# Three pairs of feature tiles in seven products in each later part's Down, with scratch tiles reused, and one unit's plain products moved

## Chip, cores and metric

One core of a Trainium2 chip. The metric is the device time of one launch in microseconds (us), less is better. TensorE (PE) multiplies, VectorE (DVE) and ScalarE (ACT) do elementwise work, GpSimd (POOL) does some of it too and issues a few DMAs, SyncE (SP) issues most DMAs.

## The reference

A trunk of two layers over 512 positions and 1024 features, float32, batch 1. Each layer has two gated feed-forwards with a mixer between them:

```python
for l in range(2):
    x = x + 0.5 * swiglu(rms_norm(x, ffn1_norm[l]), ffn1_w_gate[l], ffn1_w_up[l], ffn1_w_down[l])
    h = rms_norm(x, mix_norm[l])
    a, g, q, k, v = split(h @ w_in[l])
    # causal depthwise convolution of width 31 on a * sigmoid(g); two softmax maps of q, k with a
    # shared position bias, A1 - lam * A2, lam from four vectors lambda_q1, k1, q2, k2
    x = x + concatenate([conv_out, diff_out]) @ w_out[l]
    x = x + 0.5 * swiglu(rms_norm(x, ffn2_norm[l]), ffn2_w_gate[l], ffn2_w_up[l], ffn2_w_down[l])

def swiglu(h, w_gate, w_up, w_down):        # 1024 -> 2816 -> 1024
    return (silu(h @ w_gate) * (h @ w_up)) @ w_down
```

## The kernel before

**Layout and products.** x lies feature-major: 8 tiles of 128 features by 512 positions. Every product is made in three matmuls: weights and data are each split into a rounded part (hi, an ACT copy) and what is left (lo, a DVE subtraction), and hi·hi, hi·lo and lo·hi are summed in PSUM. Weights come by SP's DMAs into a ring (wraw), and their hi and lo into two more (whi, wlo).

**A feed-forward.** Its 2816 inner features are 22 tiles, split by PARTS into three parts. The first, 5 tiles, is done plainly: 512 columns a matmul, lines 138 to 142. The parts of 8 and 9 tiles are done in units, all of whose matmuls come from line 377. `Unit.body` writes out the order; the scheduler may interleave it. There are two kinds:

- A GateUp unit makes one inner tile: the gate and up products, as one two-by-two block product (two weight blocks for gate and for up, two halves of the positions) with seven half-width products in place of eight (the scheme of Strassen and Winograd), 84 matmuls of 256 columns. Its weights are u1, u2, g1, g2 (halves of a DMA'd tile each), and four sums of them, which POOL makes (lines 354 to 357). The first of these sums goes into a tile of the ring wraw2, called "D". The operands A, B, C and D of a unit are: u (its first half replaced by u1+u2), g, the two last sums, and the first sum.
- A Down unit makes two output tiles A = 2q and B = 2q+1 (q = 0 to 3, four units for a part). `pairs` pairs of the part's inner tiles are taken in seven half-width products each, the others plainly with 512 columns: for B into a bank of its own (`spare`, tile ps_d), for A into the unit's second bank (`plain(self.banks[1], 0)`).

**Order in a unit.** On PE a unit runs: c (weights u2u1, data t1), d (u2, t4), for Down with q > 0 the spare products, then the `rest` of the unit before (g1u1, t3), a (g1, b11), b (g2, b21), `middle` (Down's plain products for A), c (all, b22), a (g1u2u1, t2), `close`. The last of the a-products is read out by ACT into a keep copy (line 426) before `rest`, issued in the next unit, may add to the same bank. Within a unit the next one's weights are made: hi of A, B, D, C on ACT (line 363), lo on DVE (line 367), from sums that POOL made ahead.

**The data of Down.** `Gated` takes a finished GateUp tile: a hi copy (line 628) and lo (line 633), and for the first tile of a pair a held copy in float32 (line 613) and a half-tile subtraction (line 618). When the second of a pair is there, `combine` (lines 635 to 648) makes three sums of the pair and their hi and lo, into scratch named by STORE: two slots of ht, one of rb, and s0 to s2. `Halves` makes the sums of the feed-forward's input, with the same ht slots as its scratch.

**Ends.** The last Down unit of a feed-forward is followed by its `rest` and then by the mixer, by the next feed-forward, or by the end of the kernel. The call `after` starts the statistics of the next norm for an output tile, or the output's DMA.

**The start.** While x is loaded, `make_scalars` fetches the four lambda vectors of each layer (tile lamv, POOL's queue) and forms lam. `make_bias` fetches the onehot table (tile oneh, in the ring sq of two slots, which also holds the squares of the first norm).

Of the kernel before, what the change touches and what calls it, by code (L numbers as in the profile page):

```python
# [41 lines left out]
HS = SEQ // 2  # L42


PARTS = ((0, 5, 0), (5, 8, 2), (13, 9, 2))
PLAIN = PARTS[0][1]
PIN = False

# [20 lines left out]
def trunk(ctx: ExitStack, tc: tile.TileContext, xt, par, lamv, relb, onehot,  # L69
          gu1, dn1, wag, wqkv, wout, gu2, dn2, out):  # L70
    nc = tc.nc
    V, S, G, T = nc.vector, nc.scalar, nc.gpsimd, nc.tensor
# [14 lines left out]
    def bank(tag, name):  # L87
        return psum.tile([P, 512], F32, tag=tag, name=name, bufs=BANKS[tag])


    RING = {"wraw": 5, "whi": 4, "wlo": 4, "wraw2": 2, "whi2": 2, "wlo2": 2}

    def ring(tag, n=1024):
        dt = F32 if "raw" in tag else F32R
        return wp.tile([P, n], dt, tag=tag, name=tag, bufs=RING[tag])

# [197 lines left out]
    class Halves:  # L294
# [4 lines left out]
        def __init__(self, fp, pr, r):  # L299
            self.th = fp.tile([P, 3, KT // 2, HS], F32R, tag="th", name="th")  # L300
            self.tl = fp.tile([P, 3, KT // 2, HS], F32R, tag="tl", name="tl")

            self.whole = []
            free = [f"{t}{n}" for t in ("hh", "hl") for n in range(5, 9)]
            a, b = slice(0, HS), slice(HS, SEQ)
            for j in range(KT // 2):
                for k in (j, j + KT // 2):
                    h = fp.tile([P, SEQ], F32, tag=free.pop(), name="hn")
                    V.scalar_tensor_tensor(h, x[:, k, :], col(pr.l, pr.gain, k), r, op0=ALU.mult, op1=ALU.mult)
                    self.whole.append((k, h))  # L310
# [22 lines left out]
    def pinned(ins, pin=PIN):  # L333
        if pin:
            tc.keep_in_program_order(ins)
        return ins
# [4 lines left out]
    def by_two(t):  # L341
        return t.rearrange("p (n c) -> p n c", n=2)
# [150 lines left out]
    class Down(Unit):  # L493
# [6 lines left out]
        def load(self):  # L500
            A, B = 2 * self.q, 2 * self.q + 1
            whole, over, J = min(self.many, 8), max(self.many - 8, 0), self.steps * P

            def pull(raw, at, m, k, end):
                while k < end:
                    half, f = divmod(self.m0 + k, HALF)
                    b, w = m * HALF + f, 1
                    while (b + w) % 8 and k + w < end and f + w < HALF:
                        w += 1
                    c = b % 8  # L510
                    nc.sync.dma_start(raw[:, at : at + w * P], self.dn[half, b // 8][:, c * P : (c + w) * P])
# [18 lines left out]
            self.cols = {"A": whole * P, "B": whole * P, "C": 2 * J, "D": J + 2 * over * P}  # L530

        def weights(self, wt, j):
            k, b = {"u2u1": ("A", 2 * j), "u2": ("A", 2 * j + 1), "g1": ("B", 2 * j), "g2": ("B", 2 * j + 1),
# [4 lines left out]
            return self.h.get(xt, j)  # L538

        def plain(self, ps, n, first=False):  # L540
            over = max(self.many - 8, 0)
            w = [
                self.w("BA"[n], k) if k < 8 else self.w("D", self.steps + n * over + k - 8)
                for k in range(2 * self.steps, self.many)
            ]
            self.product(ps, zip(w, self.h.hh[2 * self.steps :]), first)

        def spare(self):
            self.ps = bank(("tp", "y")[self.q % 2], "ps_d")
            self.plain(self.ps, 1, first=True)  # L550
# [14 lines left out]
        def close(self):  # L565
            A, B = 2 * self.q, 2 * self.q + 1
            two, keep = by_two(self.banks[1]), self.keep
            if not self.early_free:
                self.plain(self.banks[1], 0)
            pinned(V.tensor_tensor(two, two, keep[:, 0::2], op=ALU.add))  # L570
# [4 lines left out]
            two = by_two(self.ps)  # L575
            pinned(V.tensor_tensor(two, two, keep[:, 1::2], op=ALU.subtract))
            self.into(B, two, 0.5)

        def rest(self):
            self.go(self.a, "g1u1", "t3")  # L580
            B = 2 * self.q + 1
            self.into(B, self.a.unsqueeze(1).broadcast_to([P, 2, HS]), -0.5)
            self.after(B)

    class Gated:

        STORE = (("ht", "ht", "rb"), ("s0", "s1", "s2"))

        def __init__(self, fp, pairs):
            self.fp, self.pairs = fp, pairs  # L590
            self.hh, self.sums, self.held = [], [], {}

        def part(self, tag):
            pool, bufs = (act, None) if tag == "rb" else (self.fp, 2 if tag == "ht" else None)
            return pool.tile([P, SEQ], F32R, tag=tag, name="hs", **({"bufs": bufs} if bufs else {}))

        def plain(self, n, us):
            hi = self.fp.tile([P, SEQ], F32R, tag=f"hh{n}", name="hh")
# [8 lines left out]
        def add(self, n, us, step):  # L607
            a, b = slice(0, HS), slice(HS, SEQ)
            first = self.paired(n) and n % 2 == 0
            if step == 0:  # L610
                if first:
                    self.held[n] = self.fp.tile([P, SEQ], F32, tag=("hh8", "hl8")[n // 2 % 2], name="hold")
                    pinned(S.activation(self.held[n], us, AF.Copy))
                else:
                    self.part_hi(n, us)
            if step == 1:
                if first:
                    pinned(V.tensor_tensor(us[:, b], self.held[n][:, a], self.held[n][:, b], op=ALU.subtract))
# [16 lines left out]
        def combine(self, n, us):  # L635
            if not self.paired(n) or n % 2 == 0:
                return
            a, b = slice(0, HS), slice(HS, SEQ)
            t = self.held[n - 1]
            pinned(V.tensor_tensor(t[:, b], us[:, b], t[:, b], op=ALU.subtract))  # L640
            pinned(V.scalar_tensor_tensor(t[:, a], t[:, a], -1.0, t[:, b], op0=ALU.mult, op1=ALU.subtract))
            pinned(V.scalar_tensor_tensor(us[:, a], us[:, a], -1.0, t[:, a], op0=ALU.mult, op1=ALU.subtract))
# [553 lines left out]
```

## Time and profile before

| what | value |
|---|---|
| median of 3 runs | 1791.06 us (1789.68 to 1792.72) |
| the profiled execution | 1787.99 us, of which the span is 1786.2 |
| matmul records | 11437 |
| POOL busy | 950.4 us, 53% of the span |
| weight DMAs of GateUp | 172 of 512 KB, 3.6 us each to landing |
| DMA, mean over the span | 100 GB/s |

Times of instructions come from the one profiled execution, which is shorter than each of the timed runs. A row of the chain gives start, length, engine, tile and line, and the number of instructions that follow one another (x12). A row of the timeline gives start, length, engine, line, operation, the tile written, the tiles read, shapes, and in brackets how long the engine was idle before it and for what. Matmuls are pipelined: what one costs in a stream is the length of a piece over its count, not the duration of a record.

### The profile page before, as it was taken

Reading aid. Unit: us, or ns where it says so; the run is one execution under the profiler, and the core shown is the slowest. Engines: PE = TensorE matmul, PEld = TensorE weight load, DVE = VectorE, ACT = ScalarE, POOL = GpSimd, SP = SyncE. Lnnn points to the kernel's source line nnn. Section 1 sums busy time; section 2 is a strip of 40 time slices with the busy share of each in tenths; the row PEclk is TensorE's granted clock in tenths of the full one; section 3 lists DMA queues with packets and bytes.
Section 4 is the critical chain, followed back from the end, with each engine's and each line's share of the span. In section 5 each row is a group of like instructions: output and inputs, shape, how many; then the busy total and the mean of one; then the engine's idle time right before and its main releaser. Section 6 shows DMA issues by size and latency. Waiting matters only on the chain.

```text
span 1786.2 us, 29641 instructions
## 1 busy us (share of the span) xinstructions
PE 1771.4 (99%) x11437; PEld 1608.5 (90%) x11437; DVE 1416.0 (79%) x1949; ACT 960.1 (54%) x1555; POOL 950.4 (53%) x665
## 2 busy tenths in 40 slices
PE   9999999999999999999999999999999999999998
PEld 7899999888788899999888999998877888999997
DVE  6988797768857978798668978976788588887974
ACT  5455465545844456465534654655558354554652
POOL 2275475279952166475304745742798432654750
PEclk9999999999999999999999999999999999999999
DMA  7333334423122233333332333344230232333332
GB/s 224 95 113 97 105 107 113 128 91 95 48 71 83 83 95 118 85 113 120 107 97 71 107 107 99 103 119 130 71 116 26 72 106 73 106 97 105 107 108 70
DMA packets 74222, 177.83 MB, mean 100 GB/s; under 512 B 8951, under 2 KB 30726, under 8 KB 74080
## 3 DMA queue, kind: packets, MB, share of 16 engines
q1 hardware_dynamic: 72480, 174.10, 31.9%
q8 instruction: 89, 1.46, 0.3%
q0 software_dynamic: 1312, 1.67, 0.3%
q14 instruction: 53, 0.43, 0.1%
q10 hardware_dynamic: 288, 0.16, 0.0%
HBM read 173.79 MB, written 3.42 MB: 99 GB/s over the span
## 4 chain that ended last, share of the span: by engine, by line
PE 96%; DVE 2%; ACT 1%; issue 0%; DMA 0%; SPq 0%; DVEq 0%; ACTq 0%
PE ps_pair L377 53%; PE ps_d L377 6%; PE ps_pair L141 5%; PE ps_pair L142 5%; PE ps_pair L138 5%; PE ps_d L138 2%; PE ps_d L142 2%; PE ps_d L141 2%; PE ps_sc L966 2%; PE ps_pair L842 2%; PE ps_pair L843 2%; PE ps_pair L844 2%; PE ps_out L138 1%; PE ps_out L142 1%; PE ps_out L141 1%; PE ps_v L872 1%
## 5 line engine op out<-in xcount | busy, mean ns | idle before, releaser
L367 DVE TENSOR_TENSOR wlo<-wraw,whi 128x1024 fp32r<-128x1024 f32 (+2 forms) x400 | 534.6, 1342 | 122.0 <-ACT whi L363 120.2
L363 ACT ACTIVATE whi<-wraw 128x1024 fp32r<-128x1024 f32 (+2 forms) x400 | 361.5, 909 | 354.6 <-PE ps_pair L377 188.3
L354 POOL TENSOR_TENSOR wraw<-wraw 128x512 f32<-128x512 f32 (+1 forms) x100 | 145.1, 1451 | 540.9 <-DMA wraw<-in_gu 279.4
L377 PE MATMUL ps_pair<-acth,wlo 128*128 128x256 f32 x1088 | 307.9, 283 | 0.0
L377 PE MATMUL ps_pair<-actl,whi 128*128 128x256 f32 x1088 | 307.9, 283 | 0.0
L377 PE MATMUL ps_pair<-acth,whi 128*128 128x256 f32 x1088 | 307.9, 283 | 0.0
L377 PE MATMUL ps_pair<-th,whi 128*128 128x256 f32 x816 | 231.7, 284 | 0.0
L377 PE MATMUL ps_pair<-th,wlo 128*128 128x256 f32 x816 | 230.9, 283 | 0.0
L377 PE MATMUL ps_pair<-tl,whi 128*128 128x256 f32 x816 | 230.9, 283 | 0.0
L377 PEld LDWEIGHTS ps_pair<-acth,whi 128*128 128x128 f32 x1088 | 208.9, 192 | 0.2
L377 PEld LDWEIGHTS ps_pair<-actl,whi 128*128 128x128 f32 x1088 | 208.9, 192 | 0.2
L377 PEld LDWEIGHTS ps_pair<-acth,wlo 128*128 128x128 f32 x1088 | 208.9, 192 | 0.0
L101 ACT ACTIVATE whi<-wraw 128x1024 fp32r<-128x1024 f32 (+3 forms) x124 | 122.6, 999 | 144.4 <-PE ps_pair L141 87.3
L141 PE MATMUL ps_pair<-actl,whi 128*128 128x512 f32 x448 | 174.7, 391 | 0.7 <-DVE actl L227 0.5
L142 PE MATMUL ps_pair<-acth,wlo 128*128 128x512 f32 x448 | 174.1, 390 | 0.0
L138 PE MATMUL ps_pair<-acth,whi 128*128 128x512 f32 x448 | 173.2, 392 | 0.4 <-ACT whi L101 0.4
L356 POOL TENSOR_TENSOR wraw<-wraw 128x512 f32<-128x512 f32 (+1 forms) x100 | 154.0, 1540 | 7.8
L377 PEld LDWEIGHTS ps_pair<-th,whi 128*128 128x128 f32 x816 | 156.6, 192 | 0.9
L357 POOL TENSOR_TENSOR wraw<-wraw 128x512 f32<-128x512 f32 (+1 forms) x100 | 153.2, 1532 | 7.8
L377 PEld LDWEIGHTS ps_pair<-tl,whi 128*128 128x128 f32 x816 | 156.6, 192 | 0.0
L377 PEld LDWEIGHTS ps_pair<-th,wlo 128*128 128x128 f32 x816 | 156.6, 192 | 0.0
L355 POOL TENSOR_TENSOR wraw<-wraw 128x512 f32<-128x512 f32 (+1 forms) x100 | 148.1, 1481 | 7.8
(203 smaller groups left out, 4307.5 us busy)
## 6 DMA issues: line engine op xcount, KB each, us to landing
wraw<-in_gu SPq DMA_DIRECT2D x172, 512.0 KB, 3.6
wraw<-in_wqkv SPq DMA_DIRECT2D x24, 512.0 KB, 3.6
wraw<-in_wag SPq DMA_DIRECT2D x16, 512.0 KB, 3.6
wraw<-in_wout SPq DMA_DIRECT2D x16, 512.0 KB, 3.6
wraw<-in_dn SPq DMA_DIRECT2D x60, 128.0 KB, 3.0
wraw<-in_dn SPq DMA_DIRECT2D x20, 384.0 KB, 3.3
wraw<-in_dn SPq DMA_DIRECT2D x28, 256.0 KB, 2.9
wraw<-in_dn SPq DMA_DIRECT2D x20, 320.0 KB, 3.1
```

The lines of the kernel that those rows point to most:

```text
L101: S.activation(hi, raw, AF.Copy)
L138: first = T.matmul(ps, wh, xh, start=start, stop=False)
L141: T.matmul(ps, wh, xl, start=False, stop=False)
L142: T.matmul(ps, wl, xh, start=False, stop=stop)
L354: G.tensor_tensor(d, g1, u1, op=ALU.add)
L355: G.tensor_tensor(u1, u1, u2, op=ALU.add)
L356: G.tensor_tensor(m0, u1, g1, op=ALU.add)
L357: G.tensor_tensor(m1, m0, g2, op=ALU.add)
L363: pinned(S.activation(hi[:, : self.cols[k]], self.raw[k][:, : self.cols[k]], AF.Copy), pin)
L367: pinned(V.tensor_tensor(out=lo[:, :c], in0=self.raw[k][:, :c], in1=f32(hi[:, :c]), op=ALU.subtract), pin)
L377: mm = T.matmul(ps, l, r, start=first and i == n == 0, stop=False, skip_group_check=True)
L842: T.matmul(ps[n], xh[:, t], wh, start=k == 0, stop=False)
```

## The change

- Both later parts take three pairs of inner tiles in seven products, where it was two: six of 8 and six of 9 tiles, so that two and three tiles stay plain.
- The scratch for the third pair's sums comes from tiles that exist: ht becomes one tile of three slots (`Halves` uses parts of it in turn), then rb, s0 to s4 follow, in order of demand. The list goes on with slots of ssum and sq, which three pairs don't reach.
- The ring wraw2 has one slot, where it had two.
- The ninth tile's weight columns: A's stay in D behind its sums; B's no longer fit there, since 3 + 2 tiles are more than 512 columns, and go behind the sums in C.
- In the last unit of a feed-forward, A's plain products move from `middle` to `close`, that is behind the t2 products and ahead of `rest`.
- The half-tile subtraction for the first of a pair reads one operand from PSUM, not from the held copy.
- lamv takes the slots of sq, not one of its own.
- The guards and the branch for parts that have no plain tile are never taken with these sizes.

By the order in which the changed kernel's instructions stand on each engine, the matmuls of 256 columns grow by 672 and those of 512 shrink by 384. ACT, DVE and POOL keep their order but for the added operations of the third pair. On POOL's queue the two lamv DMAs stand directly ahead of the first one of oneh, and on DVE their two reductions stand between the lo subtractions of the first weights, the second directly ahead of line 200's reduction.

```diff
-PARTS = ((0, 5, 0), (5, 8, 2), (13, 9, 2))
+PARTS = ((0, 5, 0), (5, 8, 3), (13, 9, 3))
...
-    RING = {"wraw": 5, "whi": 4, "wlo": 4, "wraw2": 2, "whi2": 2, "wlo2": 2}
+    RING = {"wraw": 5, "whi": 4, "wlo": 4, "wraw2": 1, "whi2": 2, "wlo2": 2}
...
+            ht = fp.tile([P, 2, 3, HS], F32, tag="ht", name="ht")
             for j in range(KT // 2):
...
-                t = fp.tile([P, 3, HS], F32, tag="ht", name="ht", bufs=2)
+                t = ht[:, j % 2]
...
-            pull(d, J, A, whole, self.many)
-            pull(d, J + over * P, B, whole, self.many)
             more = ring("wraw")
+            at = {"D": J, "C": 2 * J}
+            raw = {"D": d, "C": more}
+            where = ("D", "D") if J + 2 * over * P <= 512 else ("D", "C")
+            self.ninth = []
+            for n, m in enumerate((A, B)):
+                k = where[n]
+                self.ninth.append((k, at[k] // P))
+                pull(raw[k], at[k], m, whole, self.many)
+                at[k] += over * P
...
         def middle(self):
-            if self.early_free:
+            if self.early_free and not self.last:
                 self.plain(self.banks[1], 0)
...
-            if not self.early_free:
+            if not self.early_free or self.last:
                 self.plain(self.banks[1], 0)
...
-        STORE = (("ht", "ht", "rb"), ("s0", "s1", "s2"))
...
+        def part(self):
+
+            if not self.slots:
+                ht = self.fp.tile([P, 3, SEQ], F32R, tag="ht", name="hs")
+                self.slots = [lambda n=n: ht[:, n] for n in range(3)]
+                tags = [(act, "rb", None)] + [(self.fp, f"s{n}", None) for n in range(5)]
+                tags += [(tmp, "ssum", 1), (tmp, "sq", None), (tmp, "sq", None)]
...
+            return self.slots.pop(0)()
...
-                    pinned(V.tensor_tensor(us[:, b], self.held[n][:, a], self.held[n][:, b], op=ALU.subtract))
+                    pinned(V.tensor_tensor(us[:, b], self.held[n][:, a], us[:, b], op=ALU.subtract))
...
-            hi, lo, four = (self.part(tag) for tag in self.STORE[n // 2])
+            hi, lo, four = (self.part() for _ in range(3))
...
-            t = tmp.tile([P, SEQ], F32, tag="diag", name="lamv", bufs=1)
+            t = tmp.tile([P, SEQ], F32, tag="sq", name="lamv")
```

More of the change, by code (lines that the diff above doesn't have):

```diff
@@ L529, in load @@
             self.raw = {"A": u, "B": g, "C": more, "D": d}
-            self.cols = {"A": whole * P, "B": whole * P, "C": 2 * J, "D": J + 2 * over * P}
+            self.cols = {"A": whole * P, "B": whole * P, **at}
         def weights(self, wt, j):
@@ L540, in plain @@
         def plain(self, ps, n, first=False):
-            over = max(self.many - 8, 0)
+            if 2 * self.steps == self.many:
+                return
             w = [
-                self.w("BA"[n], k) if k < 8 else self.w("D", self.steps + n * over + k - 8)
+                self.w("BA"[n], k) if k < 8 else self.w(*self.ninth[n])
                 for k in range(2 * self.steps, self.many)
@@ L548, in spare @@
         def spare(self):
-            self.ps = bank(("tp", "y")[self.q % 2], "ps_d")
-            self.plain(self.ps, 1, first=True)
+            if 2 * self.steps < self.many:
+                self.ps = bank(("tp", "y")[self.q % 2], "ps_d")
+                self.plain(self.ps, 1, first=True)
         def early(self):
@@ L574, in close @@
                 self.spare()
-            two = by_two(self.ps)
-            pinned(V.tensor_tensor(two, two, keep[:, 1::2], op=ALU.subtract))
-            self.into(B, two, 0.5)
+            if 2 * self.steps < self.many:
+                two = by_two(self.ps)
+                pinned(V.tensor_tensor(two, two, keep[:, 1::2], op=ALU.subtract))
+                self.into(B, two, 0.5)
         def rest(self):
@@ L581, in rest @@
             B = 2 * self.q + 1
-            self.into(B, self.a.unsqueeze(1).broadcast_to([P, 2, HS]), -0.5)
+            if 2 * self.steps < self.many:
+                self.into(B, self.a.unsqueeze(1).broadcast_to([P, 2, HS]), -0.5)
+            else:
+                pinned(V.tensor_tensor(self.d, self.a, self.keep[:, 3], op=ALU.add))
+                pinned(V.tensor_tensor(self.a, self.a, self.keep[:, 1], op=ALU.add))
+                self.into(B, by_two(self.banks[0]), -0.5)
             self.after(B)
     class Gated:
-        STORE = (("ht", "ht", "rb"), ("s0", "s1", "s2"))
         def __init__(self, fp, pairs):
             self.fp, self.pairs = fp, pairs
[L591 to L595, printed above, removed]
+            self.hh, self.sums, self.held, self.slots = [], [], {}, []
+        def part(self):
[4 more added lines that the diff above has]
+                tags += [(tmp, "ssum", 1), (tmp, "sq", None), (tmp, "sq", None)]
+                self.slots += [
+                    lambda pool=pool, tag=tag, bufs=bufs: pool.tile(
+                        [P, SEQ], F32R, tag=tag, name="hs", **({"bufs": bufs} if bufs else {}))
+                    for pool, tag, bufs in tags
+                ]
+            return self.slots.pop(0)()
         def plain(self, n, us):
```

## The prediction

> **What bounds the kernel now.** I read the page first: its first part (busy time of each engine) and the shares of the chain that ended last.
>
> ```profile
> span 1786.2 us, 29641 instructions
> PE 1771.4 (99%) x11437; PEld 1608.5 (90%) x11437; DVE 1416.0 (79%) x1949; ACT 960.1 (54%) x1555; POOL 950.4 (53%) x665
> PE 96%; DVE 2%; ACT 1%; issue 0%; DMA 0%; SPq 0%; DVEq 0%; ACTq 0%
> ```
>
> TensorE is busy for 99% of the span and makes up 96% of the chain. So the change is worth what it saves on PE, plus the few PE stalls it closes, minus those it opens. Next the chain in order of time, for the price of both matmul widths and for the stalls:
>
> ```profile
> 90.65 87.87 PE ps_pair L377 x720
> 178.52 2.72 PE ps_d L377 x12
> ...
> 185.42 7.77 PE ps_pair L377 x54
> ...
> 328.87 3.43 PE ps_d L377 x15
> ...
> 344.18 6.91 PE ps_pair L377 x44
> 351.15 1.06 ACT whi L101
> 352.21 0.28 ACT keep L426
> 352.54 0.98 PE ps_pair L377 x6
> ...
> 1238.25 1.06 ACT whi L101
> ```
>
> The ps_d pieces are 512-wide plain products: 2.72/12 = 0.2267 us and 3.43/15 = 0.2287 us; I take 0.228. The first piece is 720 matmuls, of which 12 are plain products of the first Down unit and 708 are 256-wide: (87.87 − 2.72)/708 = 0.1203 us. The x54 piece is 42 half-width and 12 plain ones: 42 × 0.1203 + 12 × 0.228 = 7.79, and it took 7.77, so both prices hold in a mixed stream. No piece of another engine stands between these until 351.09 (344.18 + 6.91): there PE waits until 352.54 for ACT, which first makes the hi part of the mixer's next weights (1.06 us) and only then the keep copy (0.28 us) that Down's rest products need. The second layer shows the same piece at 1238.25.
>
> How much room the others have, in one stretch of GateUp and one of Down units (columns: window, length, then busy time with instruction count of PE, PEld, DVE, ACT, POOL, then clock, DMA share, GB/s):
>
> ```profile
> 213.00:303.00 90.00, 90.00 (x753) 90.00 (x752) 80.86 (x92) 54.54 (x86) 57.48 (x36) 1.00 0.38 113
> 303.00:351.00 48.00, 48.00 (x293) 43.01 (x291) 32.79 (x43) 25.40 (x41) 14.65 (x13) 1.00 0.35 109
> ```
>
> DVE is at 90% in GateUp and 68% in Down, POOL at 64% and 31%.
>
> **The third pair.** Two more feature tiles of a part go from plain to seven products. For one Down unit (two output tiles) that removes 2 tiles × 2 outputs × 3 = 12 matmuls of 512 columns and adds 7 × 3 = 21 of 256: 21 × 0.1203 = 2.526 against 12 × 0.228 = 2.736, a gain of 0.21 us. There are 4 units × 2 parts × 4 feed-forwards = 32: **−6.7 us**. With 0.2267 or 0.2287 for the wide ones it is −6.2 or −7.0. All of it is on PE, so on the path.
>
> Here a page of the Trainium skill speaks against the change. "TensorE: Matmul & The Clock Gate", section "Back-to-back issue gap", gives for a stream of weight loads and matmuls about 81 ns at 128 columns and about 131 ns at 512, so narrow products would be far from half price. An estimate from that page, by a straight line 98 ns for 256, makes it 21 × 98 − 12 × 131 = +0.49 us a unit, 15 us slower in all. The trace does not agree: 0.1203 and 0.228 us, nearly half price, and the rows decide.
>
> **The moved last products.** In the last unit of a feed-forward A's plain products (now 9: three tiles × 3) go from before the b22 and t2 products to behind t2. At both FFN1 ends they take 9 × 0.228 = 2.05 us, which is longer than the 1.45 us that PE waits there now; the copies are made meanwhile. −1.4 each, **−2.8**. If ACT came later still, up to 0.6 us of it would be covered too. The price: A's own sum now starts at the end of these products, 0.65 us behind where the keep copy ends, so the mixer's statistics of that tile come that much later (0 to +0.5 each, taken as 0, since PE has the rest products and the mixer's first plain products to do). Layer 0's FFN2 has no wait there: its rest products start without an idle remark, behind products of the next feed-forward.
>
> ```profile
> 900.42 0.40 PE L377 MATMUL ps_pair<-hs,whi 128*128 128x256 f32 x2
> ```
>
> So 0 for it. At the kernel's end the chain is
>
> ```profile
> 1780.46 0.39 ACT keep L426
> 1780.88 0.71 DVE ps_pair L570
> 1781.62 0.69 DVE x L561
> 1782.31 0.60 DVEq L1191
> ```
>
> Last products of t2 to the last update of x: 2.47 us (1780.44 to 1782.91). Afterwards t2 ends earlier by 15 plain matmuls moved or dropped for A and 6 dropped for B (21 × 0.228 = 4.79), later by 18 half-width ones of this unit and 3 of the previous rest (21 × 0.1203 = 2.53): −2.26. From there: 2.05 of plain products, then on DVE the sum (0.71) and two updates of x (0.69, 0.60), with the gaps of some hundredths between the rows 4.1 in place of 2.47: +1.63. Together −0.63, of which 0.2 stands already among the 32 units: **−0.4**.
>
> **lamv in the ring of sq.** At the start the two lamv tiles lay in a slot of their own; now they take the two slots of sq, are fetched only when the sums of squares are made, and the onehot tile, which has the same ring, must wait until they are read.
>
> ```profile
> 27.39 0.57 POOL L740 DMA_DIRECT2D oneh<-in_onehot  x1 [11.07 <-DVE ssum L239]
> 27.95 4.63 DVE L102 TENSOR_TENSOR wlo<-wraw,whi 128x1024 fp32r<-128x1024 f32 x4
> 32.49 0.69 DVE L200 TENSOR_REDUCE rowv<-ps_rows 128x4 f32<-128x512 f32 x1
> 33.47 1.04 POOL L189 TENSOR_TENSOR rs_y<-rowv,mhalf 128x4 f32<-128x4 f32 x1 [5.51 <-DVE rowv L201]
> 37.06 0.65 PE L209 MATMUL ps_spread<-ident,rs_y 128*128 128x128 f32 x4
> L761 POOL TENSOR_TENSOR lamv<-lamv x4: 309/317/322, 6.1 to 16.0; 128x64 f32<-128x64 f32 x4
> L763 DVE TENSOR_REDUCE lamd<-lamv x2: 273/279/285, 7.0 to 16.3; 128x2 f32<-128x128 f32 x2
> DMA to landing us min/median/max: 4.3/5.4/6.5
> ```
>
> The first lamv DMA issues where oneh does now, 27.39, and lands at 31.7 to 33.9; two POOL products and one reduction are 0.9. Its reduction stands on DVE between the second and the third of the four wlo, so those two (2.3 us) start after 32.6 to 34.8 and end at 34.9 to 37.1; then come the second reduction (0.28) and L200, now at 32.49, at 35.2 to 37.4: 2.7 to 4.9 later. From L200 to ps_spread there are 2.5 us of slack (rs_y ends at 34.51, PE uses it at 37.06). So PE waits 0.2 to 2.4 us, once; I take the middle, **+1.3**. Queued behind on POOL are the oneh DMAs and rs_y, on DVE the two wlo for PE's next products: all in the same wait, and paid once.
>
> **One wraw2 slot in place of two.** The "D" sums of unit n+2 (L354, POOL) may now start only when lo of D of unit n+1 (L367, DVE) has read the slot. The stretch of two GateUp units:
>
> ```profile
> 232.20 1.06 ACT L363 ACTIVATE whi<-wraw 128x1024 fp32r<-128x1024 f32 x1 [0.41 <-PE ps_pair L377]
> 242.28 1.06 ACT L363 ACTIVATE whi<-wraw 128x1024 fp32r<-128x1024 f32 x1 [1.32 <-POOL wraw L356]
> 243.25 0.37 ACT L426 ACTIVATE keep<-ps_pair 128x256 f32<-128x256 f32 x1
> 237.60 1.50 DVE L367 TENSOR_TENSOR wlo<-wraw,whi 128x512 fp32r<-128x512 f32 x1
> 244.05 1.21 DVE L367 TENSOR_TENSOR wlo<-wraw,whi 128x1024 fp32r<-128x1024 f32 x1
> 246.72 2.31 DVE L367 TENSOR_TENSOR wlo<-wraw,whi 128x1024 fp32r<-128x1024 f32 x1
> 249.62 1.12 DVE L367 TENSOR_TENSOR wlo<-wraw,whi 128x512 fp32r<-128x512 f32 x1
> 237.25 1.29 POOL L354 TENSOR_TENSOR wraw<-wraw 128x512 f32<-128x512 f32 x1 [3.77 <-DMA wraw<-in_gu]
> 238.62 1.62 POOL L355 TENSOR_TENSOR wraw<-wraw 128x512 f32<-128x512 f32 x1
> 248.03 2.17 POOL L355 TENSOR_TENSOR wraw<-wraw 128x512 f32<-128x512 f32 x1
> ...
> 325.87 0.69 DVE L367 TENSOR_TENSOR wlo<-wraw,whi 128x512 fp32r<-128x512 f32 x1 [0.82 <-ACT whi L363]
> ```
>
> A unit lasts 10.08 us (232.20 to 242.28). In the second one a pair of tiles is combined for Down, in the first not; I call them combining and light. lo D ends 6.9 us after the unit's start in the first (239.10), 8.5 in the second (250.74). L354 and L355, on which the next unit's hi A waits, take 3.0 to 3.5. Unmoved, the sums would be ready at 9.9 to 10.4 and 12.0. But the two sides now overlap: a 1024-wide lo takes 1.21 alone and 2.31 beside POOL, the 512-wide one 0.69 and 1.12 to 1.50. With the sums behind lo D, lo B and lo D run alone: about 0.8 less in the light unit (6.1) and 1.5 less in the combining one, of which about 1 is given back, since the later sums run into the next lo A (1.21 to 2.3): 8.0. So ready at 9.1 to 9.6 and 11.0 to 11.5. hi A, 1.06, and behind it on ACT the keep copy, 0.37, must end before PE starts the previous unit's rest, 24 products (2.9 us) into the next unit: the sums may take until 10.08 + 2.9 − 1.06 − 0.37 = 11.5. Just in time. Behind L354 on POOL stand L355, L356 and L357; the last two feed hi C, which ACT makes some 7 us after hi A, so nobody waits for them. I take **+0.5** in all (0 to 1), and keep the case that it is missed for the rivals.
>
> On the overlap, the Trainium skill ("SBUF — State Buffer", section "Who interferes with whom") says that VectorE and GpSimd contend only for one shared port pair, as an exclusive lock. The 1.21 and 2.31 agree.
>
> **Further operations, costed at nothing.** One more combination in each part (L640 to L647), and in Down wider sums on POOL and wider hi and lo: they lie on engines that the windows show idle for 10% (DVE, GateUp) and 32 to 69% (Down). Without that cover each would cost its own length. The subtraction that now reads PSUM gets shorter, as these two forms of one shape show:
>
> ```profile
> L618 DVE TENSOR_TENSOR ps_pair<-hold 128x256 f32<-128x256 f32 x16 | 24.4, 1522 | 0.0
> L642 DVE SCALAR_TENSOR_TENSOR ps_pair<-ps_pair,hold 128x256 f32<-128x256 f32 x16 | 6.7, 420 | 0.0
> ```
>
> 1.1 us less of DVE in each unit that has it, against 2.4 more (four half-width operations at 0.42, one full at L570's 0.71) in the one unit per part that newly combines. The ninth tile's B weights come from C: lo C ends at 326.56 (325.87 + 0.69) and would be read 6 matmuls into the ps_d run of 328.87, at 330.24: 3.7 us spare, of which the wider C takes about 0.7.
>
> **Sum.** −6.7 − 2.8 − 0.4 + 1.3 + 0.5 = −8.1. The profiled execution took 1787.99 (span 1786.2 and 1.8 around it), so about 1779.9; the runs' median, 1791.06, lies 3.1 above it, and from that it is **1783.0**. 0.2% (3.6 us) is about what a measurement of this kernel can tell from no change.
>
> **Rivals.**
> (a) Small waits in many units: the sums miss 11.5 by 0.1 to 0.3 us in the 24 combining units (3 per part, 8 parts): +2.4 to +7, and the gain is 1 to 6. For it: the margin worked out is nil. 1785 to 1790, chance 0.20, half of it within 0.2%.
> (b) Slower: lo D stays at 8.5 in the combining unit, because DVE, at 90%, doesn't turn the faster lo into an earlier one. Sums at 12.0 to 12.3, keep copy 0.5 to 0.8 us late, in 24 units: +12 to +19, 1795 to 1802. It decides from 11.5 on. Against it: L618's 1.1 us and the lifted overlap. Chance 0.13.
> (c) The C weights of the ninth tile come late, 1 us in 12 units: gain lost, 1787 to 1795. The 3.7 us speak against it. 0.06 (a third within 0.2%).
> (d) The narrow products cost more than 2.736/21 = 0.130 us where Down mixes widths. The dearest row is the x6 piece behind the stall, 0.98/6 = 0.163; at that the third pair is +22 in place of −6.7: 1812. The x54 piece speaks against it. 0.01. This is the case of the Trainium skill's "TensorE: Matmul & The Clock Gate", above.
> The forecast itself: 0.60.
>
> **How the numbers follow.** Faster: 0.60 and half of (a), 0.70. Same: 0.10 and 0.02, 0.12. Slower: 0.13, 0.04, 0.01, 0.18. Low end: wide price 0.2287 (0.3), no small wait (0.5), lamv at 0.2 (1.1), and the 1.5 us by which runs of before lie around their median (1789.68 to 1792.72): 1779.5. High end: through (a) and the near end of (c), 1791.
>
> **What the profile after would show.** Of the page, some 288 more matmul instructions. In the chain: ps_d pieces x6 of 1.37 us (part of 8) and x9 of 2.05 (part of 9) in place of 2.72 and 3.43, half-width pieces longer by 15 products; no ACT piece at both FFN1 ends; in GateUp stretches no ACT keep between PE pieces, and L354 released by DVE wlo. A PE gap of about 1.3 us near 37. It is wrong if PE idles ahead of rest in combining units (b), ahead of the third plain tile of a ps_d run (c), or if 21 half-width products take over 2.74 us (d).

## The result and the profile after

| | median | runs | ratio to before, 95% interval |
|---|---|---|---|
| before | 1790.62 us | 1789.17 to 1792.72 (6) | |
| changed | 1781.70 us | 1779.90 to 1782.79 (6) | 0.9953 (0.9942 to 0.9963) |

The changed kernel is 8.9 us faster; 8.1 were forecast (1783.0, range 1779.5 to 1791.0). One thing is needed to read single numbers below: the mean granted clock of a run lies between 0.997 and 1.000, and in most profiles it is 0.50 for 3.4 or 6.8 us inside a mixer (last section), so small differences are read in the traces, stage by stage, and not in single times.

The page of the changed kernel, first part and chain shares:

```profile
span 1778.1 us, 30234 instructions
PE 1765.5 (99%) x11725; PEld 1617.3 (91%) x11725; DVE 1394.3 (78%) x1997; ACT 986.9 (56%) x1579; POOL 965.4 (54%) x665
PE 89%; DVE 6%; issue 2%; POOL 2%; ACT 1%; DMA 0%; DVEq 0%; SPq 0%; ACTq 0%
```

There are 288 more matmuls, 9 net in each of the 32 Down units, and yet PE is busy for less time. DVE and POOL hold 8% of the chain, where it was 2%: some pieces of theirs now stand between PE's. Its chain in order of time, for the Down units and the end of layer 0's FFN1:

```profile
179.32 1.36 PE ps_d L378 x6
...
184.22 8.93 PE ps_pair L378 x69
193.16 1.39 PE ps_d L378 x6
...
328.22 2.07 PE ps_d L378 x9
330.28 9.61 PE ps_pair L378 x72
339.90 2.07 PE ps_d L378 x9
341.96 8.53 PE ps_pair L378 x63
350.50 0.23 PE ps_pair L138
```

A unit of the part of 8 takes 8.93 + 1.39 = 10.32 us (2.75 + 7.77 = 10.52 before), one of the part of 9 takes 11.68. Behind the last unit's 63 products the mixer's first product follows without a gap: the ACT pieces that stood at 351.15 and 352.21 are gone.

Where time was won and lost is read best from PE's own stages. This table has the length from the first unit product of a feed-forward to the end of the last, worked out from PE's timeline, and the tail from there to the end of the span (to about 0.05 us). The kernels e1 to e12 are the experiments below.

| kernel | FFN1, layer 0 | FFN2, layer 0 | FFN1, layer 1 | FFN2, layer 1 | tail |
|---|---|---|---|---|---|
| before | 263.02 | 267.56 | 263.02 | 262.15 | 4.32 |
| changed | 260.19 | 266.12 | 260.22 | 260.82 | 4.35 |
| e1 changed, plain products in the middle | 261.79 | 266.32 | 261.79 | 261.52 | 3.95 |
| e2 before, with the move | 261.42 | 267.32 | 261.42 | 261.42 | 4.58 |
| e4 before, one slot | 263.83 | 268.35 | 263.84 | 262.95 | 4.31 |
| e6 changed, keep copy first | 259.48 | 265.39 | 259.47 | 259.47 | 4.36 |
| e7 changed, two slots | 259.47 | 265.39 | 259.47 | 259.47 | 4.38 |
| e8 changed, slow subtraction | 260.31 | 266.23 | 260.30 | 260.96 | 4.43 |
| e9 changed, two slots, two pairs | 261.41 | 267.33 | 261.42 | 261.42 | 4.59 |
| e10 changed, two slots, slow subtraction | 259.47 | 265.39 | 259.47 | 259.47 | 4.34 |
| e11 before, keep copy first | 268.99 | 273.48 | 269.62 | 268.18 | 4.34 |
| e12 changed, two slots, keep copy first | 266.96 | 273.90 | 267.24 | 268.30 | 4.36 |

Between before and changed the four feed-forwards and the tail give −2.83, −1.44, −2.80 and −1.30: −8.4. The start (−0.2) and what lies between the feed-forwards (+0.5) make it −8.1, which is the difference of the two spans. One reading of the table needs care. At the end of layer 0's FFN2 plain products of the next feed-forward stand among the last unit products, 27 of them in the kernel before and 26 in the changed one. So 0.24 of the −1.44 is no gain, but one plain product that moved over the boundary and is part of the +0.5.

What the one slot does is seen in the middle of a GateUp stretch, at a combining unit. The hi A at the unit's start, then POOL, DVE's lo D, ACT and PE's weight load, from the timeline of the changed kernel (in brackets the idle time ahead and who ended it):

```profile
241.49 1.06 ACT L364 ACTIVATE whi<-wraw 128x1024 fp32r<-128x1024 f32 x1 [1.32 <-POOL wraw L356]
...
249.63 1.30 POOL L355 TENSOR_TENSOR wraw<-wraw 128x512 f32<-128x512 f32 x1 [5.09 <-DVE wlo L368]
251.01 2.16 POOL L356 TENSOR_TENSOR wraw<-wraw 128x512 f32<-128x512 f32 x1
248.88 0.67 DVE L368 TENSOR_TENSOR wlo<-wraw,whi 128x512 fp32r<-128x512 f32 x1
253.20 1.06 ACT L364 ACTIVATE whi<-wraw 128x1024 fp32r<-128x1024 f32 x1 [1.94 <-POOL wraw L356]
254.17 0.36 ACT L427 ACTIVATE keep<-ps_pair 128x256 f32<-128x256 f32 x1
254.58 0.19 PEld L378 LDWEIGHTS ps_pair<-th,whi 128*128 128x128 f32 x1 [0.31 <-ACT keep L427]
PEld ps_pair L378 <- ACT keep L427: 3.1, 9, 0.6
```

It is the whole loop of the prediction: lo D ends at 249.55, the sum D starts behind it, the sum for A ends at 253.17, hi A follows at once, the keep copy behind hi A ends at 254.53, and the weight load of the rest products comes 0.31 us later than the pipeline wanted. The last row, from PEld's waits, says that this happens 9 times: once in each of the eight parts, and once more in the last feed-forward.

### The profile page after: what moved, and what is told of

Same layout as the page of the kernel before. It is cut to its first block, busy times and chain, and to the rows that moved or that the text cites. A ratio compares the mean times of both kernels' runs of the same rounds, so it can differ in the third digit from the quotient of the medians.

```text
span 1778.1 us, 30234 instructions
## 1 busy us (share of the span) xinstructions
PE 1765.5 (99%) x11725; PEld 1617.3 (91%) x11725; DVE 1394.3 (78%) x1997; ACT 986.9 (56%) x1579; POOL 965.4 (54%) x665
## 3 DMA queue, kind: packets, MB, share of 16 engines
q8 instruction: 92, 1.51, 0.3%
## 4 chain that ended last, share of the span: by engine, by line
PE 89%; DVE 6%; issue 2%; POOL 2%; ACT 1%; DMA 0%; DVEq 0%; SPq 0%; ACTq 0%
PE ps_pair L378 48%; PE ps_pair L141 5%; PE ps_pair L142 5%; PE ps_pair L138 5%; PE ps_d L378 3%; DVE wlo L368 2%; PE ps_d L141 2%; PE ps_d L142 2%; PE ps_d L138 2%; PE ps_sc L990 2%; PE ps_pair L867 2%; PE ps_pair L868 2%; PE ps_pair L866 2%; PE ps_out L138 1%; PE ps_out L142 1%
## 5 line engine op out<-in xcount | busy, mean ns | idle before, releaser
L368 DVE TENSOR_TENSOR wlo<-wraw,whi 128x1024 fp32r<-128x1024 f32 (+4 forms) x400 | 510.3, 1277 | 171.9 <-ACT whi L364 171.4
L364 ACT ACTIVATE whi<-wraw 128x1024 fp32r<-128x1024 f32 (+4 forms) x400 | 373.6, 935 | 333.5 <-PE ps_pair L378 153.1
L355 POOL TENSOR_TENSOR wraw<-wraw 128x512 f32<-128x512 f32 (+1 forms) x100 | 127.8, 1278 | 554.7 <-DVE wlo L368 366.5
L357 POOL TENSOR_TENSOR wraw<-wraw 128x512 f32<-128x512 f32 (+1 forms) x100 | 169.3, 1693 | 7.9
L358 POOL TENSOR_TENSOR wraw<-wraw 128x512 f32<-128x512 f32 (+1 forms) x100 | 164.3, 1643 | 7.8
L356 POOL TENSOR_TENSOR wraw<-wraw 128x512 f32<-128x512 f32 (+1 forms) x100 | 149.9, 1499 | 7.6
```

The costliest lines, as they stand in the source:

```text
L355: G.tensor_tensor(d, g1, u1, op=ALU.add)
L356: G.tensor_tensor(u1, u1, u2, op=ALU.add)
L357: G.tensor_tensor(m0, u1, g1, op=ALU.add)
L358: G.tensor_tensor(m1, m0, g2, op=ALU.add)
L364: pinned(S.activation(hi[:, : self.cols[k]], self.raw[k][:, : self.cols[k]], AF.Copy), pin)
L368: pinned(V.tensor_tensor(out=lo[:, :c], in0=self.raw[k][:, :c], in1=f32(hi[:, :c]), op=ALU.subtract), pin)
```

## The experiments

Each ratio is to the kernel before, run on the same chip beside it; the range behind it is the 95% interval.

**e1: the move undone.** The changed kernel with the last unit's plain products ahead of b22 and t2 again:

```diff
-            if self.early_free and not self.last:
+            if self.early_free:
                 self.plain(self.banks[1], 0)
...
-            if not self.early_free or self.last:
+            if not self.early_free:
                 self.plain(self.banks[1], 0)
```

> The changed kernel, with the last unit's plain products put back before b22 and t2. If the move is worth what the prediction says, PE waits again for ACT's hi copy and keep copy at both FFN1 ends (1.4 us each) and the end of the kernel is 0.4 later: about 3.2 us of the 8.9 are lost, -5.7 against before. Rival: the mixer has the same idle time later anyway, because A's sum comes 0.65 us earlier now; then the loss is under 1 us, -8 or more.

Measured: 0.9979 (0.9970 to 0.9987), −3.8 us. The chain of e1 at layer 0's FFN1 end has its ACT piece back:

```profile
342.37 7.35 PE ps_pair L378 x53
349.79 1.06 ACT whi L101
351.17 1.33 PE ps_pair L378 x9
```

In the table 1.60 and 1.57 come back at the two FFN1 ends and 0.3 at the kernel's end, 3.5 in all against the 3.2 expected. The 0.2 at layer 0's FFN2 is the one plain product at the boundary again: from the first unit product there to the first of the next feed-forward it is 342.61 us in e1 and 342.62 in the changed kernel. In time, −5.7 was expected and −3.8 measured. The interval reaches down to −5.4, which is 8.9 less 3.5; whether the rest is more than noise isn't shown. The rival, that the mixer would idle later anyway, falls.

**e2: the move alone**, put into the kernel before (the reverse edit).

> The kernel before, with the move of the last unit's plain products alone. Here they are 15 (3.42 us) and cover the 1.45 us at both FFN1 ends; at the end of the kernel 3.42 us of them move behind t2, whose chain of DVE work is then 3.0 longer: -1.4 x 2 - 0.4 = -3.2. Rival: A's sum, 2.0 us later than the keep copy allows, delays the mixer's statistics, and 0 to -1.5 is left.

Measured: 0.9999 (0.9990 to 1.0007), no difference. At the two FFN1 ends it gains 1.60 each and at the kernel's end 0.47, 3.7 us, somewhat more than expected (the −0.24 at layer 0's FFN2 is the boundary again: 343.84 us to the next feed-forward's first unit product in the kernel before, 343.86 in e2). The chain at the FFN1 end has no ACT piece:

```profile
344.06 7.73 PE ps_pair L377 x51
352.03 0.23 PE ps_pair L141
```

More than half of what it wins is given back in a mixer. That of layer 1 takes 281.38 us between its feed-forwards, 279.13 in the kernel before, at a granted clock of 1.00 in both (layer 0's, with 0.90 to 0.93 over 40 us in this profile, tells nothing). The statistics are not late, as the rival had it: they run 6.7 us after the mixer's start in both. The first transposed attention tile is late: it comes 109.7 us after the start in before and 120.6 us in e2, because the scheduler, which places the mixer's work around the feed-forward's end, wrote the attention in another order. Here are these rows in the timelines of before and of e2 (starts of the mixers: 1240.6 and 1239.7):

```profile
1350.29 0.49 PE L987 MATMUL ps_at<-ident,e 128*128 128x128 f32 x3
```

```profile
1360.33 0.60 PE L987 MATMUL ps_at<-ident,e 128*128 128x128 f32 x4
```

In all the traces PE's products in layer 1's mixer stand in one of two orders: e2 and e9 have this one, every other kernel that of before. What is left of the gain, 1.4 us, lies within the interval of the ratio (−1.8 to +1.3 us). So both the forecast and the rival missed; and the changed kernel, whose mixers take 280.52 and 279.08, was spared this.

**e3: lamv in the ring of sq, alone**, in the kernel before (`tag="sq"` in place of `tag="diag", bufs=1`).

> The kernel before, with lamv alone put in the ring of sq. By the prediction PE's ps_bias and ps_spread run 1.3 us later than at 36.11 and 37.06. By the trace of the changed kernel, where they started at 35.93 and 36.88, they don't move by more than 0.3 us, because the scheduler put the sums of squares ahead of the weights' lo parts and so freed the ring about 2.7 us earlier.

Measured: 1.0002 (0.9992 to 1.0012). PE's rows in question, in e3's timeline:

```profile
36.28 1.02 PE L743 MATMUL ps_bias<-oneh,relb 33*4 33x512 f32 x2
37.23 0.54 PE L209 MATMUL ps_spread<-ident,rs_y 128*128 128x128 f32 x3
```

They were at 36.11 and 37.06: 0.17 later, and neither shows a wait. In the changed kernel they are even earlier. Its timeline of POOL at the start, and the landing time of lamv:

```profile
24.70 0.61 POOL L783 DMA_DIRECT2D lamv<-in_lamv  x1 [16.08 <-DVE ssum L239]
25.48 0.55 POOL L783 DMA_DIRECT2D lamv<-in_lamv  x1 [0.17 <-issue]
28.04 3.30 POOL L785 TENSOR_TENSOR lamv<-lamv 128x64 f32<-128x64 f32 x4 [2.01 <-DMA lamv<-in_lamv]
31.29 0.59 POOL L764 DMA_DIRECT2D oneh<-in_onehot  x1
DMA to landing us min/median/max: 3.2/3.2/3.3
```

The first lamv DMA issues at 24.70, not at 27.39, and lands in 3.2 us, not in 4.3 to 6.5. The reason for the earlier start is lamv itself. In the kernel before DVE stood idle for lamv's product, ahead of the sums of squares:

```profile
16.35 0.28 DVE L763 TENSOR_REDUCE lamd<-lamv 128x2 f32<-128x128 f32 x1 [2.73 <-POOL lamv L761]
```

In e3 and in the changed kernel this reduction runs only at 29.97 and 29.75, so the wait is gone and the sums come 2.5 to 2.7 us sooner. But for it and the tiny operation that goes with it (nlam), the sums stand behind the same operations on DVE in all three. They were not put ahead of lo parts, as the expectation had it.

**e4: one slot alone**, in the kernel before (`"wraw2": 1`).

> The kernel before, with one slot for wraw2 alone, the two pairs and the slow subtraction kept. 16 units combine. If the keep copy is just in time behind hi A, as predicted, 0 to +2 us. If lo D stays where it was and the sums only come behind it (rival b), 0.5 to 0.8 us in 16 units, +8 to +13.

Measured: 1.0018 (1.0009 to 1.0027), +3.3 us; each feed-forward is 0.8 longer. PEld's waits in e4:

```profile
PEld ps_pair L377 <- ACT keep L426: 6.6, 11, 1.6
```

Three of the 11 are the old ones at the ends of feed-forwards; of the waits that this view lists the kernel before has these three alone. The other eight are one for each part. It is more than the 0 to 2 expected, and far from rival (b)'s 8 to 13.

**e5, e6, e7: what the one slot costs in the changed kernel.** e5 is the changed kernel again. e6 has the keep copy pinned ahead of the next hi A on ACT, and e7 two slots:

```diff
-            self.begin()
+            self.begin(), nxt and nxt.hi("A", True)
...
-                nxt.hi("A")
...
-            pinned(S.activation(self.keep[:, 2], self.a, AF.Copy))
+            pinned(S.activation(self.keep[:, 2], self.a, AF.Copy), True)
```

```diff
-    RING = {"wraw": 5, "whi": 4, "wlo": 4, "wraw2": 1, "whi2": 2, "wlo2": 2}
+    RING = {"wraw": 5, "whi": 4, "wlo": 4, "wraw2": 2, "whi2": 2, "wlo2": 2}
...
-    ones_r = const.tile([P, P + SPACE], F32R, tag="ones_r", name="ones_r")[:, :P]
+    ones_r = const.tile([P, P], F32R, tag="ones_r", name="ones_r")[:, :P]
...
-    ones = const.tile([P, P], F32, tag="ones", name="ones")
-    G.memset(ones, 1.0)
```

> The changed kernel once more, as the base for the three others of this group: 0.995 of the time before.

> The changed kernel, with ACT made to issue the keep copy ahead of the next hi A. The changed kernel's four feed-forwards are each about 0.45 us longer than the sum of their terms. If that is the keep copy waiting behind a hi A that waits for POOL's sums, it goes: -1.8 against the changed kernel, and no weight load waits for the keep copy in GateUp. Rival: DVE or POOL are late themselves; then the wait only moves to the lo parts, and the time is the same or longer.

> The changed kernel with two slots for wraw2 again; the room comes from the padding of a constant tile and from a constant tile that nothing reads. If the one slot is the cause of the 0.45 us in each feed-forward, -1.8 against the changed kernel, as the sums no longer wait for lo D. Rival: with the sums beside lo B and lo D again DVE's operations get longer, and the third pair's work has no room: 0 or slower.

Measured: e5 0.9952 (0.9940 to 0.9965), e6 0.9929 (0.9917 to 0.9942), e7 0.9929 (0.9916 to 0.9943). The medians are 1782.89, 1778.23 and 1778.38 us: e6 and e7 both undo the wait, and gain the same. In the table the four feed-forwards shrink to the same lengths to a hundredth, by 0.72, 0.73, 0.74 and 1.35: 3.5 us, not the 1.8 expected. Neither kernel has a weight load that waits for the keep copy. In e6 the sums are as late as in the changed kernel, but the keep copy no longer stands behind them. In e7 the sums start early again. ACT's keep copy in e6, and POOL's first sum and lo D in e7, in the timelines of the same stretch:

```profile
252.01 0.38 ACT L427 ACTIVATE keep<-ps_pair 128x256 f32<-128x256 f32 x1 [0.94 <-PE ps_pair L378]
```

```profile
244.91 1.53 POOL L355 TENSOR_TENSOR wraw<-wraw 128x512 f32<-128x512 f32 x1 [2.62 <-DMA wraw<-in_gu]
248.11 1.12 DVE L368 TENSOR_TENSOR wlo<-wraw,whi 128x512 fp32r<-128x512 f32 x1
```

e6's copy waits for PE only. e7's first sum is released by its DMA, 4.7 us earlier than in the changed kernel.

**e8: the slow subtraction in the changed kernel** (`self.held[n][:, b]` in place of `us[:, b]`).

> The changed kernel with the half-tile subtraction reading both operands from the held copy again, which took 1.52 us and not 0.42. By the prediction's sum the light units have 1.9 us of room and the combining ones don't contain it: 0 to +0.5. Rival: DVE carries the 1.1 us into the combining unit, the sums there come later by as much, and 24 units lose up to 1.1 us each: +5 to +20.

Measured: 0.9952 (0.9940 to 0.9965), like e5; the feed-forwards are 0.1 longer, and the waits are as many:

```profile
PEld ps_pair L378 <- ACT keep L427: 3.5, 9, 0.6
```

**e9, e10: two slots without the third pair, and with the slow subtraction.** e9 has PARTS of before, e10 the edit of e8, both with e7's.

> The changed kernel with two slots for wraw2 and with two pairs in both parts, that is without the third pair alone. By the prediction's first term 6.7 us more than with two slots and three pairs (0.9929 of the time before): 0.9966. Each of the four feed-forwards 1.7 us longer. Rival: the third pair frees something beyond its matmuls, since each feed-forward gained 2.2 us with two slots where 1.7 was counted; then 8.5, 0.9976.

> The changed kernel with two slots for wraw2 and with the slow half-tile subtraction of the kernel before. If the 0.5 us a feed-forward that two slots and three pairs gained beyond the count is the shorter subtraction (weight loads waited 0.9 us in all in the kernel before and not at all with two slots), the time is 1 to 2 us over that with two slots. If DVE's 1.1 us lies in its slack, the same, and the 0.5 us have another cause.

Measured: e9 1.0002 (0.9993 to 1.0010), e10 0.9941 (0.9928 to 0.9955). Between them, on one chip, lie 10.6 us. As ratios both expectations for e9 missed (0.9966 and, for the rival, 0.9976). In the feed-forwards and the tail the third pair is worth 1.94, 1.94, 1.95 and 2.2, 8.0 in all. 6.7 was the prediction's term, and the rival's 8.5 is nearer. Most of the rest of the 10.6 is a mixer again: e9 has the attention order of e2 and takes 282.96 us there, e7 280.68, both with 3.4 us at half clock; and its table row is that of e2. Where the 8.0 comes from is seen in the starts of PE's ps_d runs: from one unit of the part of 8 to the next it is 10.52 in e9 and 10.32 in e7, 0.20 as counted. But from the feed-forward's first product to the first ps_d run it is 87.87 in e9 and 88.50 in e7, where the count gives +0.80 (18 half-width more, 6 plain fewer), and 108.43 and 108.51 over the second part's GateUp stretch, where it gives +0.23. So each part gains about 0.16 more, in the stretch that ends at its unit q = 0. It is a wait too short for the list of waits, ahead of the rest products that come in the unit q = 0. Here are ACT's keep copy and PE's products, first in e9, then in e7:

```profile
171.22 0.37 ACT L427 ACTIVATE keep<-ps_pair 128x256 f32<-128x256 f32 x1
171.44 0.28 PE L378 MATMUL ps_pair<-hs,wlo 128*128 128x256 f32 x1
171.64 0.39 PE L378 MATMUL ps_pair<-th,whi 128*128 128x256 f32 x1
171.86 0.28 PE L378 MATMUL ps_pair<-tl,whi 128*128 128x256 f32 x1
```

```profile
170.90 0.37 ACT L427 ACTIVATE keep<-ps_pair 128x256 f32<-128x256 f32 x1
171.84 0.28 PE L378 MATMUL ps_pair<-hs,wlo 128*128 128x256 f32 x1
171.96 0.28 PE L378 MATMUL ps_pair<-th,whi 128*128 128x256 f32 x1
```

In e9 the copy ends at 171.59, and the rest (th) starts at 171.64, 0.20 behind the product before it, and its second product 0.22 later, where 0.12 each is the pace: 0.18 us lost. With three pairs 18 products of c and d stand ahead of the rest in place of 12, the copy ends 0.7 us ahead of the first rest product, and nothing is lost. All traces of kernels with two pairs and hi A first (before, e2, e3, e4, e9) have this wait of the weight load, 0.12 us, eight times, one in each part; those with three pairs and hi A first have none. So the rival was right: the third pair frees 1.3 us beyond its products. e10's lengths are e7's, and its median, 1778.47 us, is e7's to 0.1: the shorter subtraction is worth nothing, which was the other explanation.

**e11, e12: the keep copy first, with two slots.** e11 is e6's edit in the kernel before; e12 is e6's and e7's together.

> The kernel before, with ACT made to issue the keep copy ahead of the next hi A, and nothing else. If the kernel before had small waits for the keep copy of its own, it gains 0.5 to 1.5 us in the four feed-forwards, besides 2.8 if the copy also no longer stands behind the mixer's hi copy at the FFN1 ends. If it had none in GateUp, 0 there.

> The changed kernel with two slots for wraw2 and the keep copy ahead of hi A, each of which alone gave 0.993 of the time before. If keep-first made the kernel before slower by 1.5% because its hi A, and with it lo A, B and D, come later and then run beside POOL's sums (3.27 us for lo B and lo D together, where they take 1.9 alone), two slots bring that overlap back here: some 0.5 to 1.2 us in each of the 24 combining units, 1.000 to 1.009. Rival: it was something else of the kernel before (its slow subtraction, its two pairs); then 0.993 as with either alone.

Measured: e11 1.0147 (1.0133 to 1.0161), e12 1.0123 (1.0106 to 1.0140). e11 was expected to gain and is 26 us slower; e12 is slower than its forecast of 1.000 to 1.009. Each edit alone made the changed kernel some 4.5 us faster, and both together make it some 30 us slower. The chain of e12, in a combining unit, PE's waits, and ACT's rows ahead of the next rest products:

```profile
271.89 1.79 DVE hs L670
...
274.36 3.27 DVE wlo L368 x2
...
PE ps_pair L378 <- ACT keep L427: 16.3, 14, 2.1
278.74 0.60 ACT L637 ACTIVATE hold<-ps_pair 128x512 f32<-128x512 f32 x1 [4.06 <-DVE ps_pair L486]
279.24 0.38 ACT L427 ACTIVATE keep<-ps_pair 128x256 f32<-128x256 f32 x1
```

In this stretch of the chain DVE's pieces stand where PE's stood. Pinned behind the keep copy, hi A comes later, and with it lo A, lo B and lo D. With two slots POOL's sums don't wait for them, so they run at the same time, and DVE's operations get longer: L670 takes 1.79 us here, 0.73 on average in the changed kernel, and lo B and lo D 3.27, 1.81 in e6. DVE is then late with L486, ACT's hold copy waits for it, and the keep copy, which PE waits for, stands behind the hold copy. In all DVE is busy for 1474.5 us in e12 and 1400.3 in e6, with the same 1997 instructions. The groups of the 512-wide lo parts show it (busy time, then mean ns of one), for before, changed, e7 and e12:

```profile
L367 DVE TENSOR_TENSOR wlo<-wraw,whi 128x512 fp32r<-128x512 f32 x116 | 125.6, 1083 | 18.7 <-ACT whi L363 18.3
```

```profile
L368 DVE TENSOR_TENSOR wlo<-wraw,whi 128x512 fp32r<-128x512 f32 x84 | 63.9, 761 | 8.6 <-ACT whi L364 8.6
```

```profile
L368 DVE TENSOR_TENSOR wlo<-wraw,whi 128x512 fp32r<-128x512 f32 x84 | 105.6, 1257 | 8.6 <-ACT whi L364 8.6
```

```profile
L368 DVE TENSOR_TENSOR wlo<-wraw,whi 128x512 fp32r<-128x512 f32 x84 | 119.2, 1420 | 6.8 <-ACT whi L364 6.8
```

One slot works as a barrier: POOL's sums can't start beside lo D, and lo D takes 0.76 us in place of 1.08 to 1.42 (the 116 of before include 32 of Down units). With it, keep-first gains; without it, keep-first loses. The rival, that the slow subtraction or the two pairs of the kernel before made e11 slow, falls with e12, which has neither.

## Why the prediction came out right, term by term

| term | predicted | measured | from |
|---|---|---|---|
| third pair | −6.7 | −8.0 | e9 against e7 |
| moved products, both FFN1 ends | −2.8 | −3.2 | e2 and before |
| the same at the kernel's end | −0.4 | −0.5 | e2 and before |
| the same at layer 0's FFN2 | 0 | 0 | e2 and before |
| lamv | +1.3 | 0 to +0.2 | e3 |
| one slot | +0.5 | +3.5 | changed against e7 |
| sum | −8.1 | −8.2 to −8.0 | |

What the change does was named rightly, and the sum came out; but that it came out to a tenth is luck. The third pair, the move and lamv were better than forecast by 1.3, 0.5 and 1.1 to 1.3 us, the one slot was worse by 3.0, and these cancel. Of the signs, the ps_d pieces came (1.36 to 1.39 and 2.07 us), the ACT piece at the FFN1 ends went, and POOL's first sum is released by DVE; the PE gap near 37 us did not come, and the keep copy, which was not to hold PE in GateUp, held it nine times.

- **Third pair.** The step from 10.52 to 10.32 us a unit was counted as 0.21 and measured as 0.20. The short wait for the keep copy in each part's first Down unit was not seen: it went into the price of 0.1203 us. The 87.87 us piece would have shown it: at 0.1200 from a whole GateUp unit, 10.08/84, its 708 narrow and 12 wide products come to 87.70.
- **Move.** PE's waits at the FFN1 ends go, as forecast. The term was short by 0.2 at each end: from the last product ahead of the stall to the first behind it PE's starts lie 1.63 us apart, 1.51 more than the pace and not 1.4, and the first product behind it took 0.22 us to the next, not 0.12. (By their starts the six rest products take 0.81 us, not the 0.98 of the chain; rival (d)'s 0.163 us is a reading of the chain.) That a reordered mixer could eat much of it (e2) was not among the rivals.
- **lamv.** The failed step is the start: 27.39 was taken over from the kernel before, but there the sums of squares stood behind DVE's 2.73 us wait for lamv, which the change removes, and the ring came free 2.7 us sooner. Its landing was taken at 4.3 to 6.5 us from DMAs issued in the first 10 us; here it was 3.2.
- **One slot.** The loop was worked out to tenths: lo D was to end 8.0 us after a combining unit's start and the sums at 11.0 to 11.5, just at the limit. In the trace above lo D ends 8.1 after the hi A slot at 241.49, and the sums at 11.7. So the condition of rival (a) came true, the sums missed 11.5 by 0.2, and its price, 2.4 to 7 us, holds the 3.5 that were paid; that the time stayed at the forecast is owed to the other terms. What rival (a) had wrong is that 24 units pay. In fact a part pays once, at its first combining unit: 0.36 us in length, and 0.40 in e4, with two pairs. In the later combining units of the changed kernel the keep copy ends 0.4 to 0.6 us ahead of its load. PE's delay of 0.31 can be a part of this; what gives the rest is not shown. And in the last feed-forward a second wait comes (0.56 in the load, 0.6 in the length).
- **Subtraction.** Counted as relief for DVE and as an argument against rival (b), it is worth nothing with two slots (e10) and 0.1 us a feed-forward with one (e8).
- **Rival (b)**, lo D staying at 8.5 us in every combining unit, did not come: it ended at 8.1. How little room DVE has is seen in e12: the edit that gains 4.5 us with one slot costs some 35 with two.

On the overlap of POOL and DVE the rule of the Trainium skill quoted in the prediction ("SBUF — State Buffer", section "Who interferes with whom") agrees with the groups above as far as they go: 0.76 us with the two kept apart, 1.26 and 1.42 side by side; that there is a contention they show, that it is a lock they don't. Of the Trainium skill's rule on narrow matmuls ("TensorE: Matmul & The Clock Gate", section "Back-to-back issue gap") the runs here show the opposite sign: 21 of 256 columns cost 0.20 us less than 12 of 512.

The best kernels of these runs are e7 and e6, 1778.4 and 1778.2 us, 0.9929 of the time before and 0.25% under e5, the changed kernel beside them.

## What to carry to other kernels

A wait in a steady pipeline need not be paid at each turn: here it was paid by 9 of 24 units, once in each part and twice in one, so its price should be worked out per stretch as well as per turn. A list of waits can leave out short ones: eight of 0.12 us, listed nowhere, were worth 1.3 us, and a sum of starts against the pace finds them. A buffer taken away can also order two engines that slow each other, so the cost of a slot and the gain from keeping the engines apart must be put in the same sum, and an edit that helps beside it should be tried again without it. And where a scheduler places the work, an edit at a stage's end is judged by the stages behind it too: e2 won 3.7 us in the feed-forwards and lost 2.3 of them in a mixer.

## What the runs showed of the hardware

A subtraction of 512 columns from two SBUF tiles on DVE took 0.76 us on average when POOL's sums were held behind it, and 1.42 us in e12, where they ran together; two of these lo parts, one of 1024 and one of 512 columns, took 3.27 us there and 1.81 in e6.

A narrow product of 256 columns took 0.120 us in a stream and a wide one of 512 columns 0.228, at a granted clock of 1.00; the first product behind a wait took 0.22 us to the next (e9, and the kernel before at the FFN1 end).

The granted clock of TensorE fell to 0.50 for a few us inside a mixer in every profile but those of before and changed. A window of e3 (the last three columns are clock, DMA share and GB/s):

```profile
498.00:504.50 6.50, 6.35 (x21) 5.17 (x22) 5.57 (x19) 4.57 (x14) 3.84 (x4) 0.50 0.00 0
```

It lasted 6.8 us in e1, e2, e3 and e6 and 3.4 us in the others, always between 493 and 508 us. e3, e4, e5, e7 and e9 have another stretch of 3.4 us between 1326 and 1342 us, e12 one at 723 us in a feed-forward. Its price is seen where one program ran with and without it: layer 1's mixer took 280.65 us in e5 and 279.08 in the changed kernel, 1.6 more for 3.4 us. Why it comes in some executions and not in others isn't shown.
